# The first convolution block staged with x, the normalization in the tail of the projections, row copies on ScalarE

## The chip, the cores and the metric

The kernel runs on one core of a Trainium2 chip. Its metric is the device time of one execution in microseconds (us); lower is better. The engines are named as in the profile: PE is TensorE (PEld its weight loads), DVE is VectorE, ACT is ScalarE, POOL is GpSimd, and SP is SyncE, which issues most of the transfers. A row such as "L322 DVE ... x354 | 480.8, 1408" names a line of the kernel, its engine, what it writes and reads, how many instructions there were, their busy time in us and the mean of one in ns.

## The reference, cut to what matters

One layer of a decoder works on 2048 prompt tokens and 32 sample tokens (8 sequences of 4), 1024 wide, in fp32. The normalized input is multiplied by one wide matrix; its columns feed three branches: windowed attention (q, k, v, 12 heads of 64), a convolution branch (u) and cross-attention into 256 memory tokens (qc), besides gates. What the change touches:

```
h = _rmsnorm(x, g_pre) @ w_in
qa, ka, va, za, ub, zb, qc, zc, gt = split(h)
...
k_rows, v_rows = ka, va                                  # outputs too, row by row
glu  = ub[..., :768] * sigmoid(ub[..., 768:])
full = concatenate([hist_conv, glu], axis=1)             # 30 rows of history
conv = depthwise_conv(full, conv_w)  + conv_b            # width 31, 768 channels
ob   = silu(_layernorm(conv, ln_g, ln_b))                # over the 768 channels
conv_state = full[:, -30:]
```

The branch outputs are gated, projected, merged and projected once more. The layer also returns the key and value rows and the convolution's last 30 rows.

## The kernel before

**Layout and precision.** Tokens lie along the free axis, channels along the 128 partitions. x is kept in SBUF transposed, as eight slices of 128 channels, each split into a high and a low part. A weight block is 1024 x 128; it arrives as one 512 KB transfer (`load_w`, L145), and POOL splits it into `whi` and `wlo` (`split_pool`, L55 and L56). The raw, high and low tiles have two buffers each, so the split of the next block can begin when the first matmuls of the running block no longer need the tiles of the one before it. `gemm` (L160 to L168) makes three matmuls per slice: high by high, high by low, low by high, 24 for one piece.

**Pieces.** The 2080 tokens are cut into six pieces (`CHUNKS`: 384, 384, 384, 384, 256 and 288 columns). One weight block times six pieces is a block of the first phase: 144 matmuls. The product of a piece lies in one of four PSUM tiles `g`.

**First phase (`phase_a1`, L173).** `stage_x` (L104) brings x in six groups of three or two token tiles through the pool `xst` (seven buffers): a load by SP, squares on ScalarE, a square root, a scaling on VectorE (L127), transposes on PE (L132), and the split into high and low by ScalarE and VectorE (L135, L136). While this goes on, two blocks of q run piece by piece behind it. After the staging come the convolution's taps and the bias rows. Then six rounds follow, each a convolution block u and three blocks out of the list of k, v, q and qc, and at the end what is left of the list.

- A projection block (`blk_x`, L224; `chunk`, L229) copies each piece from PSUM by ScalarE into a staging tile `st` (L239, three buffers) and stores it by SP (L248). For k and v `rows_out` (L250) also transposes the piece back on PE, VectorE copies the rows out of PSUM (L260, and the sample rows L264), and SP stores them.
- A convolution block (`blk_u`, L268) loads 30 rows of history, transposes them into `GS` (L279, L281), multiplies the gate columns (tanh on ScalarE into `gate`, L290), then the value columns, and VectorE multiplies the two into `G` (L298; samples L303). `G` and `GS` have two buffers each in the pool `cnv`.
- `conv` (L309) then runs on VectorE: one L313, 59 L322 per block in `acc`, each a multiplication by one tap with an addition, besides the sample part (L331 to L334), the state rows (L338 to L351), and one store of `acc` to the scratch `d_c`. It is written at a lower priority (`later(LAG)`, 900 instructions), so that it falls between the work of the following blocks.

**What sets the order.** A planner takes the program's instructions with their priorities, which follow the order in which they are written unless `later` shifts them, and with its own durations puts them in one queue per engine. On the chip each engine goes through its queue in that order, and waits where an operand or a buffer is not there yet.

**Memory phase (`memory`, L884).** It computes keys and values of the 256 memory tokens (`memory_kv`, L905, eight weight blocks), the cross-attention and the sample parts. Into this phase the LayerNorm of the convolution branch is woven: `conv_norm` (L655) is a generator of nine steps of 256 columns, one per memory block, the last one behind them. A step loads six slices of `d_c` (one 128 x 1536 tile), sums over them on VectorE (`tensor_reduce`, L665), sums over partitions by a matmul with ones (L667), subtracts the mean (L668), squares on ScalarE (L671), sums again (L673, L675), makes 1/sqrt (L677, then L63 to L68: a square root on ScalarE, then a reciprocal and one correction on VectorE), scales (L679), applies `ln_g` and `ln_b` on POOL (six L681), takes tanh on ScalarE (L684), finishes the swish on VectorE (L685) and stores to `d_actb`.

**Filler.** From the end of the first phase the gate blocks (`sweep`, L1075: za, zb, zc, gt, PSUM tiles `gg`) run at the lowest priority wherever PE has room: through the memory phase, the attention of 12 heads and beyond it. Their weights are loaded from ScalarE's queue. Their tanh or swish is L243, or L245 with L246 on VectorE. The last phase (`phase_c`, L1103) gates, projects and merges.

Of the kernel before, what the change touches and what calls it, by code (L numbers as in the profile page):

```python
# [26 lines left out]
EARLY = 1  # L27
IN_COLS = 9472
# [9 lines left out]
class K:  # L38
# [134 lines left out]
    def phase_a1(self, wp, blocks=None):  # L173
        tc, nc, I, O = self.tc, self.nc, self.I, self.O
        with tc.tile_pool(name="x12", side="right", bufs=1) as xpool, \
# [4 lines left out]
                tc.tile_pool(name="pst", side="right", bufs=3, space=PSUM, reuse_waits="tile") as pst:  # L180
# [17 lines left out]
            with tc.tile_pool(name="cnv", side="right", bufs=1, reuse_waits="tile") as cnv:  # L198
                ws.append(self.load_w(wp, self.win(CQ + 128), 8, rp=self.wr))
                for cs, js in [(c, j) for c in (CHUNKS[:1], CHUNKS[1:2], CHUNKS[2:3], CHUNKS[3:4], CHUNKS[4:]) for j in range(2)]:  # L200
                    for s, n in cs:
                        self.chunk("q", js, s, n, ws[js], stg, psg, "g", pst)
                order = []
                rest = [("k", j) for j in range(6)] + [("v", j) for j in range(6)] + \
                       [("q", j) for j in range(2, 6)] + [("qc", j) for j in range(4)]
                for j in range(6):
                    order += [("u", j)] + rest[:3]
                    rest = rest[3:]
                order += rest
                for kind, j in order:  # L210
                    if blocks is not None and (kind, j) not in blocks:
                        continue
                    if kind == "u":
                        gs = self.blk_u(j, wp, stg, cnv, psg, pst)
# [7 lines left out]
                assert not out  # L222
                self.early = {("za", j): self.load_w(wp, self.win(CZA + 128 * j), 8, rp=self.wr) for j in range(EARLY)}
    def blk_x(self, kind, j, wp, stg, psg, pst):  # L224
        w = self.load_w(wp, self.win(self.BASE[kind] + j * 128), 8, rp=self.wr)
        for s, n in CHUNKS:
            self.chunk(kind, j, s, n, w, stg, psg, "g", pst)

# [21 lines left out]
    def rows_out(self, kind, j, s, n, st, stg, pst):  # L250
# [9 lines left out]
        nc.vector.tensor_copy(ro[:, :nt, :], p[:, :nt * 128].rearrange("p (t c) -> p t c", c=128))  # L260
# [7 lines left out]
    def blk_u(self, j, wp, stg, cnv, psg, pst):  # L268
        nc, I, O = self.nc, self.I, self.O
        G = cnv.tile([128, 16, 130], F32, name="G", bufs=2)  # L270
        GS = cnv.tile([128, 8, 34], F32, name="GS", bufs=2)
        nc.gpsimd.memset(G[:, :, 0:2], 0.0)

        st_in = cnv.tile([120, 2, 128], F32, name="st_in")
# [9 lines left out]

        w = self.load_w(wp, self.win(CUB + EB + j * 128), 8, rp=self.wr)
# [6 lines left out]
        for s, n in CHUNKS:  # L292
            th = gate[:, s:s + n]
            pa = psg.tile([128, 512], F32, name="g")
            self.gemm(pa[:, :n], w, [self.x_at(k, s, n) for k in range(8)])
            m = min(n, S - s)
            r0 = s // 128
            nc.vector.scalar_tensor_tensor(G[:, r0:r0 + m // 128, 2:130],  # L298
                                           th[:, :m].rearrange("p (r i) -> p r i", i=128), 1.0,
                                           pa[:, :m].rearrange("p (r i) -> p r i", i=128),  # L300
                                           op0=ALU.add, op1=ALU.mult)
            if m < n:
                nc.vector.scalar_tensor_tensor(GS[:, :, 30:34],  # L303
                                               th[:, m:n].rearrange("p (b t) -> p b t", t=4), 1.0,
                                               pa[:, m:n].rearrange("p (b t) -> p b t", t=4),
# [1002 lines left out]
```

## Time and profile before

| what | value |
|---|---|
| time, median of 3 runs | 3155.59 us (3150.18 to 3156.21) |
| profiled execution | 3154.4 us, span 3152.6 us |
| mean granted TensorE clock | 0.979 |
| busy share of PE, DVE, ACT, POOL | 95%, 64%, 36%, 43% |
| HBM traffic | 455 MB, mean 144 GB/s |
| first phase | from the start to the first filler matmul at 868.7 us |

The span runs from the first to the last instruction. Busy time of an engine leaves out its waits; matmuls are pipelined, and a "busy" PE at a lowered clock does less in the same time. The views by stretches therefore give the granted clock beside the busy time. The view of waits names for each idle time of PE the operation that ended it.

### The profile page before, as it was taken

The page shows a single profiled execution, that of the slowest core. Times are in us where ns is not written, and L with a number is a line of the kernel's source. Part 1 is how long each engine was busy: PE and PEld are TensorE (multiplying, and loading weights), DVE is VectorE, ACT ScalarE, POOL GpSimd, SP SyncE. Part 2 cuts the span into 40 slices and gives each one's busy share as a digit, 9 for nine tenths or more (in the row PEclk, how much of TensorE's full clock was granted, in tenths as well). Part 3 has the DMA queues.
Part 4 walks back from the last instruction along what each step waited for, and adds up shares of the span by engine and source line. Part 5 has one row for each costly group of instructions (what it writes and reads, how often), then busy time and mean ns, then how long its engine had stood idle before and what let it go on. Part 6 is the DMA issues. An engine that isn't in the chain of part 4 may idle for free.

```text
span 3152.6 us, 55374 instructions
## 1 busy us (share of the span) xinstructions
PE 3000.2 (95%) x20705; PEld 2839.9 (90%) x20705; DVE 2014.8 (64%) x3734; ACT 1124.2 (36%) x2835; POOL 1350.4 (43%) x1048
## 2 busy tenths in 40 slices
PE   7999999999987999999999999989899979999998
PEld 6899999999987999998999999989898967787897
DVE  5297797796677926465546766666656457556563
ACT  5010010010132433243437575656565523222221
POOL 0121221142356537444256565667676433233240
PEclk9899999999999999999999999999999989999999
DMA  7232222211265454477454656576555487657561
GB/s 250 85 103 80 80 60 61 63 62 50 81 182 167 135 153 144 147 219 239 151 139 116 161 123 163 128 185 150 156 143 152 109 279 227 223 168 227 161 197 53
DMA packets 532218, 454.66 MB, mean 144 GB/s; under 512 B 118191, under 2 KB 458581, under 8 KB 531137
## 3 DMA queue, kind: packets, MB, share of 16 engines
q1 hardware_dynamic: 357502, 335.36, 36.2%
q10 hardware_dynamic: 169840, 105.02, 11.7%
q0 software_dynamic: 4608, 10.75, 1.2%
q8 instruction: 164, 2.69, 0.4%
q14 instruction: 104, 0.85, 0.1%
HBM read 332.96 MB, written 118.04 MB: 143 GB/s over the span
## 4 chain that ended last, share of the span: by engine, by line
PE 70%; DMA 12%; DVE 7%; issue 4%; POOL 3%; ACT 2%; SPq 1%; ACTq 0%; DVEq 0%; POOLq 0%
PE g L166 8%; PE g L167 8%; PE g L168 8%; PE gg L166 6%; PE gg L168 6%; PE gg L167 6%; PE pg L168 3%; PE pg L166 3%; PE pg L167 3%; PE pt L571 2%; DMA cb<-d_cf 2%; PE y L1180 2%; PE y L1179 2%; PE y L1178 2%; PE o L598 1%
## 5 line engine op out<-in xcount | busy, mean ns | idle before, releaser
L166 PE MATMUL gg<-x0h,whi 128*128 128x256 f32 (+1 forms) x2560 | 747.9, 292 | 25.9 <-DVE st L246 12.2
L168 PE MATMUL gg<-x0h,wlo 128*128 128x256 f32 (+1 forms) x2560 | 741.8, 290 | 0.1
L167 PE MATMUL gg<-x0l,whi 128*128 128x256 f32 (+1 forms) x2560 | 741.1, 290 | 0.0
L55 POOL TENSOR_SCALAR whi<-wraw 128x1024 fp32r<-128x1024 f32 x162 | 242.7, 1500 | 928.5 <-PE g L167 524.1
L166 PEld LDWEIGHTS gg<-x0h,whi 128*128 128x128 f32 x2560 | 493.2, 193 | 35.0 <-DVE st L246 13.7
L167 PEld LDWEIGHTS gg<-x0l,whi 128*128 128x128 f32 x2560 | 493.5, 193 | 2.2 <-issue 0.5
L168 PEld LDWEIGHTS gg<-x0h,wlo 128*128 128x128 f32 x2560 | 493.2, 193 | 2.2 <-POOL wlo L56 0.3
L322 DVE SCALAR_TENSOR_TENSOR acc<-G,cw,acc 128x1536 f32<-128x1536 f32 (+15 forms) x354 | 480.8, 1408 | 0.3
L56 POOL TENSOR_TENSOR wlo<-wraw,whi 128x1024 fp32r<-128x1024 f32 x162 | 417.0, 2575 | 9.4 <-PE gg L168 0.2
L155 POOL TENSOR_TENSOR clo<-craw,chi 128x768 fp32r<-128x768 f32 (+1 forms) x96 | 174.1, 1815 | 346.0 <-ACT chi L154 329.8
L627 ACT ACTIVATE P<-T,stm 128x128 f32<-128x128 f32 (+1 forms) x576 | 260.8, 455 | 141.0 <-DVE stm L625 94.8
L239 ACT ACTIVATE st<-g 128x384 f32<-128x384 f32 (+1 forms) x132 | 60.2, 461 | 570.7 <-PE g L168 550.7
L166 PE MATMUL pg<-ac,chi 128*128 128x512 f32 (+1 forms) x640 | 229.4, 359 | 16.6 <-ACT chi L154 8.7
L625 DVE CUSTOM_DVE_ANT_0 T<-s,bias 128x128 f32<-128x128 f32 (+1 forms) x576 | 191.5, 357 | 80.8 <-PE s L617 47.0
L167 PE MATMUL pg<-ac,chi 128*128 128x512 f32 (+1 forms) x640 | 228.8, 358 | 6.3 <-DVE ac L1198 6.3
L168 PE MATMUL pg<-ac,clo 128*128 128x512 f32 (+1 forms) x640 | 227.6, 357 | 3.6 <-POOL clo L155 3.6
L576 DVE TENSOR_TENSOR pl<-pt,ph 128x512 fp32r<-128x512 f32 x240 | 155.6, 652 | 52.4 <-ACT ph L575 48.9
L168 PE MATMUL g<-x0h,wlo 128*128 128x384 f32 x544 | 184.3, 339 | 2.9 <-POOL wlo L56 2.9
L166 PE MATMUL g<-x0h,whi 128*128 128x384 f32 x544 | 183.6, 338 | 2.6 <-ACT st L239 2.3
L167 PE MATMUL g<-x1l,whi 128*128 128x384 f32 x544 | 186.0, 342 | 0.0
L167 PE MATMUL g<-x0l,whi 128*128 128x384 f32 x544 | 185.8, 342 | 0.0
L168 PE MATMUL g<-x1h,wlo 128*128 128x384 f32 x544 | 185.8, 342 | 0.0
(330 smaller groups left out, 7425.0 us busy)
## 6 DMA issues: line engine op xcount, KB each, us to landing
wraw<-in_w_in ACTq DMA_DIRECT2D x119, 512.0 KB
d_g<-st ACTq DMA_DIRECT2D x168, 128.0 KB
cb<-d_cf SPq DMA_DIRECT2D x72, 256.0 KB
g<-d_g SPq DMA_DIRECT2D x72, 256.0 KB
wraw<-in_w_in SPq DMA_DIRECT2D x35, 512.0 KB
kvc<-in_cache_k_win SPq DMA_DIRECT2D x8, 1536.0 KB
kvc<-in_cache_v_win SPq DMA_DIRECT2D x8, 1536.0 KB
raw<-d_q SPq DMA_DIRECT2D x48, 256.0 KB
```

The lines of the kernel that those rows point to most:

```text
L55: nc.gpsimd.tensor_scalar(hi, raw, 1.0, 1.0, op0=ALU.mult, op1=ALU.mult)
L56: nc.gpsimd.tensor_sub(lo, raw, hi.bitcast(F32))
L155: nc.gpsimd.tensor_sub(lo, raw, hi.bitcast(F32))
L166: nc.tensor.matmul(ps, hi[:, k, :], h, start=k == 0, stop=False)
L167: nc.tensor.matmul(ps, hi[:, k, :], l, start=False, stop=False)
L168: nc.tensor.matmul(ps, lo[:, k, :], h, start=False, stop=k == kb - 1)
L322: nc.vector.scalar_tensor_tensor(a3[:, lo:hi], G[:, src:src + hi - lo, 2 - m:130 - m], w, a3[:, lo:hi], op0=ALU.mult, op1=ALU.add)
L571: nc.tensor.transpose(t[:, 128 * x:128 * x + 128], pc, self.ident)
L576: nc.vector.tensor_tensor(pl[:, :w], t[:, :w], ph[:, :w].bitcast(F32), op=ALU.subtract)
L625: nc.vector.tensor_tensor_reduce(sc[:, :w], t[:, o:o + w], bias[:, 256 - w:256], 1.0, 3.0e38, ALU.add, ALU.min, m)
L627: nc.scalar.activation(P[:, o:o + w], sc[:, :w], AF.Exp, bias=m, scale=-1.0, accum_out=self.stl[:, col:col + 1])
L1178: nc.tensor.matmul(y[:m, c, :], ah[:, ts_], bh[:, cs], start=k == 0, stop=False)
```

## The change

It has four edits.

1. **The first convolution block goes with the staging of x.** In place of the two q blocks, the gate and value columns of u0 are multiplied piece by piece as x arrives. Its tanh goes to a staging tile `st` in place of `gate`. `xst` has six buffers in place of seven. `G` and `GS` live in two pools of one buffer each, one of them opened ahead of the staging; blocks take them in turn (`gated`).
2. **The order.** After u0 its convolution follows at the lower priority as before, then u1 with two blocks of the list, u2 with two, and so on to u5. Twelve blocks (v4, v5, six q, four qc) are left for the end: 72 pieces. The history rows are written by `states`, and the two zero columns of `G` are cleared by POOL at the first value piece.
3. **The normalization** leaves the memory phase. It gets a step after piece 28 of the last 72 and after every fifth from there (28, 33, ..., 68: nine steps). Its tiles are the convolution's: `G` and `GS` of both pools, `acc` and `gate`; its PSUM tiles are those of the transposes (`tr`). The sums over six slices are additions (five of 256 columns for the mean; one of 768 and two of 256 for the squares) in place of the two `tensor_reduce`.
4. **Row copies.** The copy of key and value rows out of PSUM (L260) is done by ScalarE in place of VectorE; the small copy of sample rows (L264) stays.

```diff
-            with tc.tile_pool(name="xst", side="right", bufs=7) as xst:
+            g0 = ctx.enter_context(tc.tile_pool(name="cng", side="right", bufs=1, reuse_waits="tile"))
+            with tc.tile_pool(name="xst", side="right", bufs=6) as xst:
...
-                ws = [self.load_w(wp, self.win(CQ), 8, rp=self.wr)]
+                ws = [self.load_w(wp, self.win(CUB + EB), 8, rp=self.wr)]
...
-                ws.append(self.load_w(wp, self.win(CQ + 128), 8, rp=self.wr))
-                for cs, js in [(c, j) for c in (CHUNKS[:1], CHUNKS[1:2], CHUNKS[2:3], CHUNKS[3:4], CHUNKS[4:]) for j in range(2)]:
-                    for s, n in cs:
-                        self.chunk("q", js, s, n, ws[js], stg, psg, "g", pst)
+                self.gpools = (g0, cnv)
+                ws.append(self.load_w(wp, self.win(CUB), 8, rp=self.wr))
+                first = self.gated(0)
+                for s, n in CHUNKS:
+                    pb = psg.tile([128, 512], F32, name="g")
+                    self.gemm(pb[:, :n], ws[0], [self.x_at(k, s, n) for k in range(8)])
+                    th = stg.tile([128, 384], F32, name="st")
+                    nc.scalar.activation(th[:, :n], pb[:, :n], AF.Tanh, scale=0.5)
+                    self.values(*first, s, n, ws[1], th, psg)
...
-                       [("q", j) for j in range(2, 6)] + [("qc", j) for j in range(4)]
+                       [("q", j) for j in range(6)] + [("qc", j) for j in range(4)]
                 for j in range(6):
-                    order += [("u", j)] + rest[:3]
-                    rest = rest[3:]
+                    order += [("u", j)] + (rest[:2] if j else [])
+                    rest = rest[2:] if j else rest
                 order += rest
+                ln = self.conv_norm(cnv, pst)
+                self.ticks = 0
+                def tick():
+                    self.ticks += 1
+                    if self.ticks >= NORM0 and (self.ticks - NORM0) % NORM1 == 0:
+                        next(ln, 0)
...
-                        self.blk_x(kind, j, wp, stg, psg, pst)
+                        self.blk_x(kind, j, wp, stg, psg, pst, tick if (kind, j) in rest else None)
...
+                for _ in ln:
+                    pass
...
-        nc.vector.tensor_copy(ro[:, :nt, :], p[:, :nt * 128].rearrange("p (t c) -> p t c", c=128))
+        nc.scalar.activation(ro[:, :nt, :], p[:, :nt * 128].rearrange("p (t c) -> p t c", c=128), AF.Copy)
...
+    def gated(self, j):
+        pool = self.gpools[j % 2]
+        G = pool.tile([128, 16, 130], F32, name="G")
+        GS = pool.tile([128, 8, 34], F32, name="GS")
+        return G, GS
...
+    def values(self, G, GS, s, n, w, th, psg):
+        nc = self.nc
+        pa = psg.tile([128, 512], F32, name="g")
+        self.gemm(pa[:, :n], w, [self.x_at(k, s, n) for k in range(8)])
...
+        if s == 0:
+            nc.gpsimd.memset(G[:, :, 0:2], 0.0)
+        nc.vector.scalar_tensor_tensor(G[:, r0:r0 + m // 128, 2:130],
...
-    def conv_norm(self, lp, ps):
+    def conv_norm(self, cnv, ps):
...
-            x = lp.tile([128, 6, W], F32, name="c", bufs=3)[:, :, :n]
+            G, GS = self.gated(s // W)
+            x = six(G.rearrange("p r i -> p (r i)"))
...
-            nc.vector.tensor_reduce(sm, x.rearrange("p j n -> p n j"), axis=AX.X, op=ALU.add)
-            p = ps.tile([128, 512], F32, name="str")[:, :n]
+            sm = GS.rearrange("p b w -> p (b w)")[:, :n]
+            nc.vector.tensor_add(sm, x[:, 0], x[:, 1])
+            for j in range(2, 6):
+                nc.vector.tensor_add(sm, sm, x[:, j])
+            p = ps.tile([128, 512], F32, name="tr")[:, :n]
...
-            nc.vector.tensor_reduce(sm, sq.rearrange("p j n -> p n j"), axis=AX.X, op=ALU.add)
-            p = ps.tile([128, 512], F32, name="sco")[:, :n]
-            nc.tensor.matmul(p, ones, sm, start=True, stop=True)
+            nc.vector.tensor_add(sq[:, 0:3], sq[:, 0:3], sq[:, 3:6])
+            nc.vector.tensor_add(sq[:, 0], sq[:, 0], sq[:, 1])
+            nc.vector.tensor_add(sq[:, 0], sq[:, 0], sq[:, 2])
+            p = ps.tile([128, 512], F32, name="tr")[:, :n]
+            nc.tensor.matmul(p, ones, sq[:, 0], start=True, stop=True)
...
-            rs = self.rsqrt(lp, var, [128, W], "ln", n)
+            nc.scalar.activation(sd, var, AF.Sqrt)
+            nc.vector.reciprocal(r, sd)
...
-                KT, VV = self.memory_kv(mp, kp, wp, ps, ln)
-            for _ in ln:
-                pass
+                KT, VV = self.memory_kv(mp, kp, wp, ps)
...
-            next(ln, 0)
```

More of the change, by code (lines that the diff above doesn't have):

```diff
@@ L1 @@
-from contextlib import contextmanager
+from contextlib import ExitStack, contextmanager
 import numpy as np
@@ L179, in phase_a1 @@
                 tc.tile_pool(name="psg", side="right", bufs=4, space=PSUM, reuse_waits="tile") as psg, \
-                tc.tile_pool(name="pst", side="right", bufs=3, space=PSUM, reuse_waits="tile") as pst:
+                tc.tile_pool(name="pst", side="right", bufs=3, space=PSUM, reuse_waits="tile") as pst, \
+                ExitStack() as ctx:
             for th in (1, 2):
@@ L213, in phase_a1 @@
                     if kind == "u":
-                        gs = self.blk_u(j, wp, stg, cnv, psg, pst)
+                        gs = first if j == 0 else self.gated(j)
+                        self.states(j, cnv, pst, gs[1])
+                        if j:
+                            self.blk_u(j, wp, cnv, psg, *gs)
                         with self.later(LAG):
@@ L266, in rows_out, with states @@
             nc.sync.dma_start(o[:, j * 128:(j + 1) * 128], ro[:NS, nt, :])
[L268 to L272, printed above, removed]
+    def gated(self, j):
[3 more added lines that the diff above has]
+        return G, GS
+    def states(self, j, cnv, pst, GS):
+        nc, I = self.nc, self.I
         st_in = cnv.tile([120, 2, 128], F32, name="st_in")
@@ L292, in blk_u @@
         for s, n in CHUNKS:
[L293 to L300, printed above, removed]
-                                           op0=ALU.add, op1=ALU.mult)
[L302 to L305, printed above, removed]
-                                               op0=ALU.add, op1=ALU.mult)
-        return G, GS
+            self.values(G, GS, s, n, w, gate[:, s:s + n], psg)
+    def values(self, G, GS, s, n, w, th, psg):
+        nc = self.nc
+        pa = psg.tile([128, 512], F32, name="g")
+        self.gemm(pa[:, :n], w, [self.x_at(k, s, n) for k in range(8)])
+        m = min(n, S - s)
+        r0 = s // 128
+        if s == 0:
+            nc.gpsimd.memset(G[:, :, 0:2], 0.0)
+        nc.vector.scalar_tensor_tensor(G[:, r0:r0 + m // 128, 2:130],
+                                       th[:, :m].rearrange("p (r i) -> p r i", i=128), 1.0,
+                                       pa[:, :m].rearrange("p (r i) -> p r i", i=128),
+                                       op0=ALU.add, op1=ALU.mult)
+        if m < n:
+            nc.vector.scalar_tensor_tensor(GS[:, :, 30:34],
+                                           th[:, m:n].rearrange("p (b t) -> p b t", t=4), 1.0,
+                                           pa[:, m:n].rearrange("p (b t) -> p b t", t=4),
+                                           op0=ALU.add, op1=ALU.mult)
     def conv(self, j, cnv, pst, G, GS):
@@ L652, in o_out @@
             nc.vector.tensor_add(d, f(O), f(tmp))
-    def conv_norm(self, lp, ps):
+    def conv_norm(self, cnv, ps):
         nc = self.nc
-        ones = lp.tile([128, 128], F32, name="ones")
+        ones = cnv.tile([128, 128], F32, name="ones")
         nc.vector.memset(ones, 1.0)
@@ L682, in conv_norm @@
                                         op0=ALU.mult, op1=ALU.add)
-            t = lp.tile([128, 6, W], F32, name="sq", bufs=1)[:, :, :n]
+            t = six(gate)
             nc.scalar.activation(t, x, AF.Tanh, scale=0.5)
```

25 lines of the change are left out of this document (16 added, 9 removed).

## The prediction

> **What bounds the kernel now.** I read the page first, then engine busy time in stretches of 50 us, then TensorE's waits in the stretch that the stretches single out, then the groups of instructions there and in the first phase. The page's head:
>
> ```profile
> span 3152.6 us, 55374 instructions
> PE 3000.2 (95%) x20705; PEld 2839.9 (90%) x20705; DVE 2014.8 (64%) x3734; ACT 1124.2 (36%) x2835; POOL 1350.4 (43%) x1048
> ```
>
> TensorE (PE) is busy 95% of the span. The change removes no matmul, so the time can only move by TensorE's idle time and by the clock it is granted. Where both are bad, by stretches (columns: stretch, its length, busy time of PE, PEld, DVE, ACT and POOL, granted clock, DMA share, GB/s):
>
> ```profile
> 650.00:700.00 50.00, 44.79 (x283) 44.06 (x281) 49.93 (x42) 5.54 (x12) 31.27 (x4) 1.00 0.21 66
> 700.00:750.00 50.00, 50.00 (x321) 50.00 (x320) 24.49 (x23) 4.05 (x9) 7.48 (x4) 1.00 0.16 54
> ...
> 850.00:900.00 50.00, 39.66 (x245) 37.62 (x245) 24.11 (x30) 11.16 (x19) 13.46 (x8) 0.87 0.52 163
> 900.00:950.00 50.00, 45.02 (x370) 44.20 (x368) 40.40 (x39) 15.01 (x26) 31.82 (x31) 1.00 0.48 141
> 950.00:1000.00 50.00, 39.11 (x280) 37.40 (x280) 37.15 (x31) 14.86 (x22) 28.01 (x25) 0.86 0.50 148
> 1000.00:1050.00 50.00, 44.07 (x348) 42.32 (x349) 40.74 (x64) 20.46 (x42) 35.80 (x32) 1.00 0.62 199
> 1050.00:1100.00 50.00, 46.95 (x384) 45.81 (x383) 46.72 (x90) 23.29 (x57) 24.53 (x25) 1.00 0.40 122
> 1100.00:1150.00 50.00, 48.43 (x387) 47.27 (x386) 19.43 (x29) 20.34 (x33) 22.98 (x23) 1.00 0.52 158
> ...
> 2550.00:2600.00 50.00, 33.53 (x118) 24.66 (x117) 32.61 (x39) 18.09 (x25) 14.34 (x10) 0.83 0.91 298
> ```
>
> The six stretches from 850 to 1150 us, where the normalization runs, leave PE idle 300 − 263.2 = 36.8 us. Two of them also have a lowered clock: at most 39.66 × 0.13 + 39.11 × 0.14 = 10.6 us of slower matmuls. What PE waited for between 840 and 1160 us (total us, times, longest), and below the "..." one row of the same view over the whole program:
>
> ```profile
> PE sco L675 <- DVE sm L673: 14.9, 5, 9.0
> PE gg L166 <- DVE st L246: 10.1, 9, 1.8
> PE str L667 <- DVE sm L665: 4.5, 5, 1.4
> PE gg L166 <- POOL whi L55: 3.9, 1, 3.9
> ...
> PE gg L166 <- DVE st L246: 12.2, 12, 1.8
> ```
>
> Rows 1 and 3 are the normalization's ones-matmuls waiting for VectorE's sums, 19.4 us. Row 2 is filler waiting for VectorE's gate step (L246): 10.1 of the program's 12.2 us of it fall in these 320 us, behind the normalization's long VectorE operations. Its groups there:
>
> ```profile
> L685 DVE SCALAR_TENSOR_TENSOR c<-sq,c 128x1536 f32<-128x1536 f32 (+1 forms) x9 | 35.3, 3926 | 21.9 <-ACT sq L684 21.9
> L681 POOL TENSOR_SCALAR c<-c,vecs 128x256 f32<-128x256 f32 (+1 forms) x54 | 28.4, 542 | 12.0 <-DVE c L679 6.7 <-DVE sl L1005 5.4
> L673 DVE TENSOR_REDUCE sm<-sq 128x256 f32<-128x1536 f32 (+1 forms) x9 | 23.5, 2613 | 9.9 <-ACT sq L671 9.9
> L665 DVE TENSOR_REDUCE sm<-c 128x256 f32<-128x1536 f32 (+1 forms) x9 | 23.2, 2577 | 0.7 <-DMA c<-d_c 0.7
> L63 ACT ACT_TABLE_LOAD x9 | 11.5, 1283 | 17.1 <-DVE var L677 11.8 <-DVE ml L926 4.8 <-ACT st L243 0.4
> L675 PE MATMUL sco<-sm,ones 128*128 128x256 f32 (+1 forms) x18 | 7.0, 479 | 14.9 <-DVE sm L673 14.9
> L667 PE MATMUL str<-sm,ones 128*128 128x256 f32 (+1 forms) x18 | 6.8, 463 | 6.1 <-DVE sm L665 4.5 <-DVE mss L917 1.5
> ```
>
> **Part one: the normalization leaves the memory phase.** Gone there are 19.4 us of direct waits and the 10.1 behind them, 29.5 together, and of the 10.6 us of clock I take 6, because the wait for the first filler weights (row 4) is there too and stays. That is −35.5; the bounds are −19.4 (only the direct waits go) and −47.4 (all 36.8 idle and all 10.6 of clock).
>
> The nine steps come back in the tail of the first phase. The 7.0 + 6.8 us of matmuls move and are neither saved nor added. Per step five 256-wide additions replace L665's 2.6 us and three additions replace L673's; the trace has no such addition, and between 128x256 on POOL at 542 ns and the reductions themselves the chain gets from about 1 us shorter to nothing. VectorE hides it: the convolutions are then over, and a step's VectorE work, 35.3 + 23.5 + 23.2 over nine plus the short ones, some 13 us, fits between steps five pieces apart, about 20 us. What is not hidden is the order: ScalarE's square root with its table load (1283 ns) and POOL's six L681 (3.3 us) are in each chain, PE takes its queue in order, and behind a ones-matmul that comes too early stands a whole piece of projection, and behind that the weights' buffers. Bounds: 0, and the 29.5 us of before; I take 13, two thirds of the direct 19.4, since no L246 stands behind VectorE there and the tail's stretch 700 to 750 leaves VectorE half free.
>
> The tail has to begin after the last convolution. That one ends in the row below at 839.4 us now. With one projection block less per convolution (24.7 us each by the two rows at 298.04 and 322.73 further down) and a first block that goes with x, it should end near 839 − 5 × 24.7 − 46 = 670. The filler starts at 868.7 us, and 45 of the 72 pieces (3.9 us each: two blocks of six between the rows at 777.05 and 823.00 below) lie from the first step to there, so the first step falls at about 693: some 20 us of margin, in which the 1 MB store of that convolution also has to land.
>
> ```profile
> 829.74 9.64 DVE L322 SCALAR_TENSOR_TENSOR acc<-G,cw,acc 128x640 f32<-128x640 f32 x8
> ...
> L166 PE MATMUL gg<-x0h,whi x24: 279/283/385, 868.7 to 879.7; 128*128 128x256 f32 x24
> ```
>
> **Part two: denser convolutions, and the row copies on ScalarE.** VectorE's groups in the first phase (110 to 870 us):
>
> ```profile
> L322 DVE SCALAR_TENSOR_TENSOR acc<-G,cw,acc 128x1536 f32<-128x1536 f32 (+15 forms) x354 | 480.8, 1408 | 0.3
> L260 DVE COPY ro<-tr 128x384 f32<-128x384 f32 (+1 forms) x72 | 35.7, 496 | 0.0
> L331 DVE TENSOR_TENSOR prod<-GS,cw 128x124 f32<-128x124 f32 x48 | 21.4, 504 | 0.0
> L298 DVE SCALAR_TENSOR_TENSOR G<-gate,g 128x384 f32<-128x384 f32 (+1 forms) x36 | 18.4, 510 | 146.5 <-PE g L168 146.5
> ```
>
> One convolution with its gating is (480.8 + 21.4 + 18.4) / 6 = 86.8 us, some 90 with the small ones. A cycle is now four blocks instead of five, 2 × 24.7 + 2 × 23.0 = 95 us. With the copies (12 × 0.5 = 6 us) VectorE would not fit, without them it just does, with 5 us to spare. ScalarE takes them for nothing: it is busy 5.54 us of 50 above, and the matmul behind L239 has three more PSUM tiles.
>
> But the copies did one thing more. POOL splits each block's weights (L55, then L56), and while VectorE runs L322 without a break, L55 does not get through (start, duration):
>
> ```profile
> 298.04 2.93 POOL L55 TENSOR_SCALAR whi<-wraw 128x1024 fp32r<-128x1024 f32 x1 [20.30 <-PE g L167]
> ...
> 322.73 2.69 POOL L55 TENSOR_SCALAR whi<-wraw 128x1024 fp32r<-128x1024 f32 x1 [18.43 <-PE g L167]
> ...
> 657.08 21.74 POOL L55 TENSOR_SCALAR whi<-wraw 128x1024 fp32r<-128x1024 f32 x1 [18.76 <-PE g L167]
> ...
> 683.12 2.95 POOL L55 TENSOR_SCALAR whi<-wraw 128x1024 fp32r<-128x1024 f32 x1
> ...
> 777.05 7.79 POOL L55 TENSOR_SCALAR whi<-wraw 128x1024 fp32r<-128x1024 f32 x1 [18.42 <-PE g L167]
> ...
> 823.00 17.29 POOL L55 TENSOR_SCALAR whi<-wraw 128x1024 fp32r<-128x1024 f32 x1 [17.00 <-PE g L167]
> ```
> ```profile
> 655.38 52.16 DVE L322 SCALAR_TENSOR_TENSOR acc<-G,cw,acc 128x768 f32<-128x768 f32 x38
> ...
> 683.21 0.45 PE L168 MATMUL g<-x0h,wlo 128*128 128x384 f32 x1 [2.95 <-POOL wlo L56]
> ```
>
> In the key and value blocks, with six copies each, L55 takes under 3 us; in the query blocks of now, which have none, it took 21.74, 2.95, 7.79 and 17.29. The 21.74 made PE late: 2.95 us at its first wlo, so that a wait up to 18.8 would have cost nothing, and with what followed from it idle 50 − 44.79 = 5.2 us in that stretch. The change makes every key and value block under a convolution like that. With about three weight splits per cycle that now lie in a run of L322 without a gap, for five cycles and a bit, some 16 splits are exposed; at one long wait in four of 5.2 us that is 21 us. The small operations of the convolution (L331 and its neighbours) can break the runs as the copies did, which the query blocks at 657 no longer had, since they were done by then. I take 8. Bounds: 0, and half of the splits, 42.
>
> The Trainium skill, "SBUF — State Buffer", section "SBUF: two separate sides", says that VectorE and GpSimd share one port pair as an exclusive lock, held for a whole instruction, by a VectorE operation with two SBUF inputs as well. The trace agrees, with 21.74 us of L55 behind 38 of L322. By that rule an operation with one input, or one that reads PSUM, opens the lock as the copies do.
>
> **Part three: the first block with x.** Two gemms per piece stay two gemms. Six buffers in place of seven hold just two groups of three tiles; the seventh let one tile of the next group go a release earlier. ScalarE gets a tanh between the square roots, so up to nine table loads of 1283 ns in its chain to the next group's scale. PE waited in this stretch for the scaled tiles already:
>
> ```profile
> PE tr L132 <- DVE xt L127: 9.9, 2, 6.0
> ...
> 48.84 1.28 SPq L117 DMA_DIRECT2D xt<-in_x_prompt  x3
> ```
>
> The bounds are 0 and 12 (all loads in the open, 11.5, or this wait doubled); I take +5: in four groups the third tile is issued behind two others of its batch (1.28 us for three), some 1 us late, and one table load in the open. The Trainium skill, "ScalarE: Activation LUTs", section "What ACT_TABLE_LOAD costs", counts a switch of tables at about 2.66 us with its drain; by it, an estimate, nine would be 24 us and this term about 11, not 5. The trace shows the 1283 ns and no row for a drain.
>
> **Part four: the end.** Filler that the shorter memory phase does not use is left for the time after attention. There the last row of the stretches has PE idle 16.5 us of 50. I take −6 between 0 and −16.5.
>
> **The sum.** −35.5 + 13 + 8 + 5 − 6 = −15.5 us against the profiled execution's own 3154.4, which gives 3138.9. That execution is 1.2 us under the median shown, 3155.6, so the forecast is **3140 us** on the median.
>
> **The rivals.**
>
> 1. *POOL is shut out* (slower). The place is the whole of the convolutions' time; the price is 5.2 us per long L55; it decides from about the eighth long wait on. Half of the 16 splits give 42 us in place of 8: −15.5 + 34 = +18.5, so 3174. For it: 21.74 and 17.29 of four. Against it: the 2.95 inside the same run of L322, and the small operations.
> 2. *The stalls move along* (no change). PE waits for the nine steps in the tail as it did in the memory phase, 29.5 instead of 13: −15.5 + 16.5 = +1, so 3157. For it: the chain of each step is as long as before, and the 20 us margin before the first step; a convolution that ends later puts PE behind it. Against it: VectorE is free there, and the fillers' L246 is not.
> 3. *A larger gain*. The tail costs 3, starvation 2, the start 2, and the end gives all 16.5: −35.5 + 3 + 2 + 2 − 16.5 = −45, so 3111. For it: VectorE is half free in the tail. Against it: the end's stretch has DMA at 0.91, which filler does not shorten.
>
> **How the numbers follow.** The forecast has 0.45, the first rival 0.17, the second 0.20, the third 0.18. The forecast's own range is 3132 to 3154: a third of each term's way to its bounds, added in squares, −8 and +14. A difference of 0.2%, 6.3 us, is about what can be told from no change. Faster (under 3149) holds the third rival and most of the forecast, 0.60; no change the second and the rest of the forecast, less what of the second lies over 3162, 0.22; slower the first and that, 0.18. For 8 in 10 the range goes from 3110 to 3170: the far half of the third rival and the far half of the first lie outside.
>
> **What would show it.** Right: PE idle between the first filler and 250 us later falls from 36.8 to some 8 us; L55 stays under 18.8 us in nearly all blocks; the ones-matmuls' own waits in the tail sum to 13. Wrong: many L55 over 18.8 with PE waiting for wlo (rival one); PE's waits at the two ones-matmuls near 20 us again, or the first load of the normalization waiting for the last convolution's store (rival two); PE's wait for scaled tiles of x well over 9.9 us. The forecast fails as a whole if the memory phase shows other waits of the same size where the normalization was.

## The result and the profile after

The changed kernel takes 3132.2 us (median) beside 3153.8 us before (five executions of each): the ratio is 0.9938 with a 95% interval of 0.9915 to 0.996, some 20 us faster. One execution of the changed kernel took 9279.7 us and is left out of the ratio. Run again later (`e12_after_again`, further down) it took 3130.1 beside 3150.8, a ratio of 0.9937 (0.9918 to 0.9955). The profiled execution took 3126.5 us, the fastest of those compared (up to 3140.9), so the stages below are read against the 3154.4 of the profiled one before, 28 us more.

The head of the page after, and then busy time by stretches (columns as in the prediction):

```profile
span 3124.7 us, 55530 instructions
PE 2989.5 (96%) x20705; PEld 2831.7 (91%) x20705; DVE 1951.8 (62%) x3716; ACT 1166.3 (37%) x2917; POOL 1390.9 (45%) x1048
```
```profile
500.00:550.00 50.00, 47.08 (x297) 46.51 (x295) 50.00 (x45) 3.65 (x8) 24.66 (x5) 1.00 0.09 25
...
800.00:850.00 50.00, 46.25 (x288) 45.28 (x287) 33.04 (x36) 19.64 (x25) 17.48 (x18) 1.00 0.42 129
850.00:900.00 50.00, 49.86 (x328) 49.15 (x327) 30.55 (x53) 21.10 (x31) 12.85 (x21) 1.00 0.42 135
900.00:950.00 50.00, 42.86 (x331) 41.73 (x330) 15.58 (x29) 10.86 (x23) 39.67 (x29) 0.90 0.63 174
950.00:1000.00 50.00, 50.00 (x411) 49.29 (x410) 17.52 (x46) 13.35 (x39) 31.89 (x28) 1.00 0.51 154
1000.00:1050.00 50.00, 49.64 (x390) 48.02 (x388) 28.95 (x70) 21.51 (x58) 18.39 (x17) 1.00 0.47 146
1050.00:1100.00 50.00, 50.00 (x400) 47.42 (x399) 34.19 (x86) 20.53 (x61) 37.50 (x36) 1.00 0.51 154
...
2400.00:2450.00 50.00, 41.42 (x300) 40.39 (x299) 13.61 (x8) 6.34 (x15) 32.44 (x19) 0.93 0.86 237
...
2550.00:2600.00 50.00, 44.70 (x179) 33.98 (x179) 37.31 (x42) 17.55 (x25) 23.89 (x13) 0.97 0.91 294
```

The memory phase, in which PE was busy 39 to 48 us of 50, is full but for its first stretch. In return PE has small gaps under the convolutions and in the tail, and a new one near 2400, where attention ends. The rows below show what PE waited for in the changed kernel between 690 and 1160 us (besides two waits of 0.4 us) and, under the "...", between 110 and 690 us. Lines after L25 are numbered anew: L710 is the ones-matmul for the mean, once L667; L56 and L57 split the weights, once L55 and L56; L357 is the tap, once L322; L334 is the gating, once L298; L263 is the copy to `st` and L280 the transposes behind it, once L239 and L256; L270 is once L246.

```profile
PE tr L710 <- DVE GS L708: 5.9, 4, 2.1
PE tr L970 <- DVE mt L966: 6.7, 2, 5.9
...
PE g L167 <- DVE G L334: 4.8, 2, 3.4
PE tr L280 <- ACT st L263: 4.0, 4, 1.5
```

The taps of all convolutions and the filler's matmuls, by tile (count, shortest, median and longest in ns, first and last start in us):

```profile
L357 DVE SCALAR_TENSOR_TENSOR acc<-G,cw,acc x354: 327/1399/4293, 119.8 to 674.8; 128x1792 f32<-128x1792 f32 x12, 128x1664 f32<-128x1664 f32 x12, 128x1536 f32<-128x1536 f32 x12, 128x1408 f32<-128x1408 f32 x12
...
L167 PE MATMUL gg<-x0h,whi x2560: 274/283/582, 893.4 to 2532.4; 128*128 128x256 f32 x173, 128*128 128x288 f32 x24
```

The last tap starts at 674.8 us, the first filler matmul at 893.4.

**Losses by stage.** PE's work is nearly the same in every complete kernel here (span less losses is 2948 to 2956 us in the rows below), so I add up what it loses: its idle time, and its busy time multiplied by what is missing of the granted clock, over stretches of 10 us. The stages end at 110 us, at 690 us, and then at milestones of PE's own rows: the first filler matmul, the first matmul of the sample attention, the first and the last score of attention, and the first matmul of the last phase. In us:

| kernel | start | convolutions | tail | memory | sample | attention | filler after it | last phase | sum |
|---|---|---|---|---|---|---|---|---|---|
| before | 33.4 | 5.2 | 0.0 | 47.9 | 12.0 | 53.8 | 3.9 | 44.5 | 200.7 |
| after | 32.8 | 11.9 | 6.1 | 10.5 | 18.6 | 47.8 | 13.8 | 31.5 | 173.0 |
| after, second profile | 34.5 | 11.6 | 8.1 | 9.6 | 21.3 | 48.1 | 9.9 | 32.3 | 175.4 |
| e8: staging and order only | 32.6 | 12.4 | 0.0 | 46.5 | 22.0 | 48.9 | 7.3 | 43.7 | 213.3 |
| e5: all but the normalization's place | 33.7 | 11.7 | 0.0 | 45.4 | 21.0 | 53.8 | 6.1 | 46.8 | 218.4 |
| e1: all but the copies on ScalarE | 35.1 | 12.5 | 13.6 | 22.5 | 18.8 | 47.1 | 16.7 | 35.1 | 201.4 |
| e2: only the copies on ScalarE | 29.1 | 34.8 | 4.2 | 49.3 | 10.3 | 53.2 | 1.6 | 43.2 | 225.7 |

The two first rows differ by 27.7 us, and the spans by 27.9: the sum closes.

### The profile page after: what moved, and what is told of

It reads as the page before. It is cut to its first block, busy times and chain, and to the rows that moved or that the text cites. A ratio compares the mean times of both kernels' runs of the same rounds, so it can differ in the third digit from the quotient of the medians.

```text
span 3124.7 us, 55530 instructions
## 1 busy us (share of the span) xinstructions
PE 2989.5 (96%) x20705; PEld 2831.7 (91%) x20705; DVE 1951.8 (62%) x3716; ACT 1166.3 (37%) x2917; POOL 1390.9 (45%) x1048
## 3 DMA queue, kind: packets, MB, share of 16 engines
q10 hardware_dynamic: 169840, 105.02, 11.7%
## 4 chain that ended last, share of the span: by engine, by line
PE 54%; DMA 9%; DVE 3%; POOL 2%; issue 2%; ACT 1%; SPq 1%; ACTq 0%; DVEq 0%; POOLq 0%
PE gg L167 8%; PE gg L169 8%; PE gg L168 8%; PE pg L169 3%; PE pg L168 3%; PE pg L167 3%; PE pt L606 3%; PE y L1224 2%; PE y L1225 2%; PE y L1223 2%; DMA cb<-d_cf 2%; PE o L633 2%; PE s L651 2%; PE s L652 2%; PE o L632 2%
## 5 line engine op out<-in xcount | busy, mean ns | idle before, releaser
L56 POOL TENSOR_SCALAR whi<-wraw 128x1024 fp32r<-128x1024 f32 x162 | 285.3, 1762 | 821.8 <-PE g L168 467.6
L357 DVE SCALAR_TENSOR_TENSOR acc<-G,cw,acc 128x1536 f32<-128x1536 f32 (+15 forms) x354 | 479.2, 1413 | 0.2
L57 POOL TENSOR_TENSOR wlo<-wraw,whi 128x1024 fp32r<-128x1024 f32 x162 | 411.9, 2543 | 8.9
L167 PE MATMUL pg<-ac,chi 128*128 128x512 f32 (+1 forms) x640 | 227.4, 357 | 12.4 <-ACT chi L155 5.2
L167 PE MATMUL g<-x1h,whi 128*128 128x384 f32 x544 | 185.2, 344 | 1.1 <-ACT x1h L136 1.1
```

The source lines that it names most:

```text
L56: nc.gpsimd.tensor_scalar(hi, raw, 1.0, 1.0, op0=ALU.mult, op1=ALU.mult)
L57: nc.gpsimd.tensor_sub(lo, raw, hi.bitcast(F32))
L167: nc.tensor.matmul(ps, hi[:, k, :], h, start=k == 0, stop=False)
L357: nc.vector.scalar_tensor_tensor(a3[:, lo:hi], G[:, src:src + hi - lo, 2 - m:130 - m], w, a3[:, lo:hi], op0=ALU.mult, op1=ALU.add)
```

## The experiments

Each ratio is against the kernel before on the same chip.

**The changed kernel again.**

> The changed kernel once more, on the chip of the three runs beside it, with a second profile: 3132 us, 15 to 22 under the kernel before. Its losses by stage are to come out within a few us of the first profile; a stage that does not was chance there.

3130.1 us, 0.9937 (0.9918 to 0.9955). Its losses are in the third row of the table: every stage is within 4 us of the first profile. So a difference of 2 or 3 us in one stage says nothing here; one of 6 is more than these two profiles differ by.

**The parts, one at a time.** Three runs leave out one or two of the edits. The first has the normalization back in `memory`, with the code it had before:

```diff
-                ln = self.conv_norm(cnv, pst)
+                ln = iter(())
...
+            ln = self.conv_norm(lp, lps)
...
-                KT, VV = self.memory_kv(mp, kp, wp, ps)
+                KT, VV = self.memory_kv(mp, kp, wp, ps, ln)
+            for _ in ln:
+                pass
```

> The changed kernel with the normalization back in the memory phase, in the form it had before (tensor_reduce, its own buffers, a step per memory block); staging, order and copies as changed. Theory one (the place of the normalization is the gain): the memory phase loses its 35 to 40 us again and the tail saves 6, and with the changes further on that gives 15 to 30 us more than the changed kernel, 3147 to 3162 us. Theory two (the shorter cycle and the copies bring the gain): 3 to 10 us more than the changed kernel, 3135 to 3142.

3176.7 us, 1.0097 (1.0069 to 1.0125): slower than before, and 1.6% slower than the changed kernel. Theory one holds, with a size that was too small (3147 to 3162): the memory phase loses 45.4 in place of 10.5, and the last phase 46.8 in place of 31.5. The waits in its memory phase are the old ones:

```profile
PE gg L167 <- DVE st L270: 10.3, 4, 5.7
PE str L702 <- DVE sm L700: 8.5, 6, 2.1
PE sco L710 <- DVE sm L708: 7.5, 4, 3.5
```

The second has, on top of this, the row copies on VectorE again (the diff of `e1` below), so that only the staging and the order are left:

> Only the first two edits: u0 in the staging and the order of u with two blocks each; the normalization in the memory phase as before, row copies on VectorE. Theory one (the copies' 18 us in the changed kernel come from a convolution chain that ends after the first normalization step): without steps in the tail a late chain costs nothing, and this is within 5 us of the run with the copies on ScalarE and the normalization in the memory phase, and near the kernel before, 3147 to 3158. Theory two (copies on VectorE cost in the convolutions themselves): 12 to 20 us slower than that run, 3162 to 3175.

3168.7 us, 1.006 (1.0044 to 1.0076). It is 8 us faster than the run with the copies on ScalarE, a little more than the 5 of theory one, and nothing like the 12 to 20 slower of theory two. But both are above the kernel before: the first two edits alone cost 0.6%. Theory two had the time (3162 to 3175), but for another reason. By the table these two edits lose 7 us more under the convolutions and 10 in the sample part, where the wait for KTh (5.1 us) is longer than before, and the first filler matmul comes 10 us later.

The third is the changed kernel with the copies back:

```diff
-        nc.scalar.activation(ro[:, :nt, :], p[:, :nt * 128].rearrange("p (t c) -> p t c", c=128), AF.Copy)
+        nc.vector.tensor_copy(ro[:, :nt, :], p[:, :nt * 128].rearrange("p (t c) -> p t c", c=128))
```

> The changed kernel with the 72 row copies back on VectorE, all else as changed. Theory one (VectorE's room): in the changed trace VectorE is busy 45 to 50 us of every 50 between 150 and 650 us; 60 copies of 0.5 us under the convolutions add 30 us to a chain that has about 10 to spare, so the last convolution ends some 20 to 30 us after 677 us, the value blocks' L334 stand behind it and the first normalization step comes late: 5 to 20 us slower than the changed kernel, 3137 to 3152. Theory two (POOL's way in): the copies out of PSUM let POOL's split of the weights through, its longest waits of 9 to 14 us fall to 3, VectorE loses nothing: same as the changed kernel or up to 8 us faster, 3124 to 3132.

3150.3 us, 1.0006 (0.9993 to 1.0019): theory one. POOL's L56 does fall to 4 us and less in every block, and it does not help, since the loss under the convolutions stays (12.5 for 11.9). The chain is 36 us late, and the tail and the start of the memory phase pay (13.6 and 22.5 for 6.1 and 10.5). PE's waits from 110 to 1216 us, then the taps, the last one now at 711.2 us:

```profile
PE tr L970 <- DVE mt L966: 12.9, 2, 10.8
PE tr L710 <- DVE GS L708: 11.3, 3, 7.5
```
```profile
L357 DVE SCALAR_TENSOR_TENSOR acc<-G,cw,acc x354: 328/1399/4304, 123.3 to 711.2; 128x1792 f32<-128x1792 f32 x12, 128x1664 f32<-128x1664 f32 x12, 128x1536 f32<-128x1536 f32 x12, 128x1408 f32<-128x1408 f32 x12
```

So the copies on ScalarE gain 0.7% where the normalization stands behind the convolutions. Where it does not they seem to lose 0.4% (1.0097 against 1.006), but those two intervals overlap.

**The copies alone, in the kernel before.** The reverse of the last diff, and nothing else:

> The kernel before with the row copies on ScalarE and nothing else changed. Theory one: VectorE waits 146 us for values in that phase anyway, so nothing is gained, and the split of weights waits 9 to 14 us instead of 3 without reaching PE: 3154, within 5 us. Theory two (the first rival of the prediction): splits now wait for the end of a run of L322 and some of them over 18.8 us, so PE waits for weights in several key and value blocks: 10 to 40 us slower, 3164 to 3194.

3178.0 us, 1.0086 (1.0073 to 1.0099): theory two by the time, not by its mechanism. L55 is shut out for 20.4 us in each of the next three convolutions and 10.41 in the first (its 21.76 later was there before, too), but PE waits for weights only once, for 3.0 us, as it did before the edit (2.95). PE waits for ScalarE. The waits of PE between 110 and 900 us:

```profile
PE tr L256 <- ACT st L239: 28.5, 3, 9.8
PE g L168 <- POOL wlo L56: 3.0, 1, 3.0
```

One of the three, engine by engine (start, duration):

```profile
295.37 20.40 POOL L55 TENSOR_SCALAR whi<-wraw 128x1024 fp32r<-128x1024 f32 x1 [20.31 <-PE g L167]
315.86 4.25 POOL L56 TENSOR_TENSOR wlo<-wraw,whi 128x1024 fp32r<-128x1024 f32 x1
...
296.00 0.42 SPq L248 DMA_DIRECT2D d_k<-st  x1
320.13 0.38 SPq L150 DMA_DIRECT2D wraw<-in_w_in  x1
320.61 0.53 SPq L262 DMA_DIRECT2D out_k_win_p<-ro  x1
...
325.36 0.49 ACT L260 ACTIVATE ro<-tr 128x384 f32<-128x384 f32 x1 [15.76 <-DMA out_k_win_s<-ro]
325.75 0.93 ACT L239 ACTIVATE st<-g 128x384 f32<-128x384 f32 x2
...
326.29 0.90 PE L256 MATMUL tr<-ident,st 128*128 128x128 f32 x3 [9.81 <-ACT st L239]
...
302.62 0.27 DVE L264 COPY ro<-tr 32x128 f32<-32x128 f32 x1
302.83 24.34 DVE L322 SCALAR_TENSOR_TENSOR acc<-G,cw,acc 128x640 f32<-128x640 f32 x17
```

The split ends at 320.11. Until then it holds the raw weights' buffer, so the next weight load waits at the head of SP's queue (320.13), and every store behind it waits, too, from 296.42 on. The row tiles `ro` are not stored, so ScalarE stands at its copy for 15.76 us; the piece's own L239 is queued behind that copy, and PE needs its tile. While the copies were on VectorE, ScalarE's queue could not be stopped by `ro`.

**The same with the weight loads off SP's queue.**

```diff
-        w = self.load_w(wp, self.win(self.BASE[kind] + j * 128), 8, rp=self.wr)
+        w = self.load_w(wp, self.win(self.BASE[kind] + j * 128), 8, q=self.nc.gpsimd, rp=self.wr)
...
-        w = self.load_w(wp, self.win(CUB + EB + j * 128), 8, rp=self.wr)
+        w = self.load_w(wp, self.win(CUB + EB + j * 128), 8, q=self.nc.gpsimd, rp=self.wr)
...
-        w = self.load_w(wp, self.win(CUB + j * 128), 8, rp=self.wr)
+        w = self.load_w(wp, self.win(CUB + j * 128), 8, q=self.nc.gpsimd, rp=self.wr)
```

> The kernel before with row copies on ScalarE (the run that took 3178), and the weight loads of the first phase's blocks issued from POOL's queue in place of SP's. Theory one (the queue): a late split keeps the raw buffer, the next weight load waits for it at the head of SP's queue, and the stores behind it keep the tiles that ScalarE and then PE need; without that load on SP's queue the 28.5 us at the transposes' wait for ScalarE vanish, and the time is 3145 to 3158. Theory two (PE waits for the weights themselves, or ScalarE for VectorE): the waits stay and it is 3168 to 3180.

3163.8 us, 1.0046 (1.0031 to 1.0062). The 28.5 us are gone, and the loss under the convolutions is 5.9 in place of 34.8, near the 5.2 of the kernel before, although L55 is still shut out for 20.4 us three times. So the path through SP's queue is shown. The time lies 6 us above what theory one gave: the memory phase loses 54.6 in place of 49.3, and the three stages behind it 2 to 5 us more each; why is open. In the changed kernel the same edit was tried:

> The changed kernel with the weight loads of the first phase's blocks issued from POOL's queue. Theory one (the queue): of the 12 us lost between 110 and 690 us the 4 at the transposes' wait for ScalarE go, and a few with them: 2 to 8 us faster than the changed kernel, 3124 to 3130. Theory two (POOL pays for issuing, or a load that waits for POOL's turn comes late for PE): 3 to 15 us slower, 3135 to 3147.

3162.5 us, 1.0039 (1.0026 to 1.0052): slower, as theory two had it, but by 30 us over the changed kernel in place of 3 to 15, and not by its reason. The wait of 4.0 at the transposes goes. But one split is now shut out for 30.38 us (what it had waited for before that was PE, not its load), and PE waits for both of its results, 9.0 us: the prediction's first rival as it was written. Why that split came to stand behind a longer run of taps is open. The convolutions lose 21.3 us in place of 11.9; the rest of the 26.8 us by which the profiles' losses differ is spread over the other stages. PE between 110 and 690 us, and the split:

```profile
PE g L167 <- DVE G L334: 6.0, 2, 3.3
PE g L167 <- POOL whi L56: 5.7, 1, 5.7
PE g L169 <- POOL wlo L57: 3.3, 1, 3.3
```
```profile
601.92 30.38 POOL L56 TENSOR_SCALAR whi<-wraw 128x1024 fp32r<-128x1024 f32 x1 [10.61 <-PE g L168]
```

**How near the changed kernel is to that.** Its convolutions are written 700 in place of 900 instructions behind (`LAG = 700`):

> The changed kernel with convolutions written 700 instead of 900 instructions behind. Theory one (VectorE is full through the convolutions, so their order hardly matters): losses between 110 and 690 us stay near 12, within 5 us of the changed kernel. Theory two (the gating L334 that now stands behind a run of L357 for 4.8 us comes later still): 6 to 15 us slower, 3138 to 3147.

3156.4 us, 1.0017 (1.0004 to 1.0031): slower by about 25 us, more than either theory, and not by L334. It is the queue again: L56 is shut out for up to 25.33 us, the next weight load stands at the head of SP's queue for 26.7, ScalarE's copy waits 18.7 for the store of a row tile, and PE waits 25.4 us for ScalarE's tile (second fence, 110 to 1000 us).

```profile
277.57 25.33 POOL L56 TENSOR_SCALAR whi<-wraw 128x1024 fp32r<-128x1024 f32 x1 [20.39 <-PE g L168]
```
```profile
PE tr L280 <- ACT st L263: 25.4, 5, 12.8
```

**What the normalization itself costs.** Its steps only load and store their columns; the convolution branch goes on unnormalized. In the changed kernel, then in the kernel before:

```diff
             nc.sync.dma_start(x, self.d_c[:, :, s:s + n].rearrange("j p n -> p j n"))
+            if True:
+                nc.sync.dma_start(self.d_actb[:, :, s:s + n].rearrange("j p n -> p j n"), x)
+                yield
+                continue
```

> The changed kernel with the normalization's arithmetic left out: its steps only load their columns and store them to the scratch again, so the convolution branch goes on unnormalized. Theory one: the normalization costs in the tail its 13.8 us of matmuls and about 6 us of idle PE: 18 to 24 us faster than the changed kernel, 3108 to 3114. Theory two (it also sets the end of the phase and disturbs the first filler): 30 to 40 us faster, 3092 to 3102.

> The kernel before with the normalization's arithmetic left out, loads and stores kept. Theory one: in the memory phase it costs the 13.8 us of matmuls and the 30 to 37 us of stalls and clock that the prediction gave it: 43 to 51 us faster than before, 3103 to 3111, so that the move itself is worth the difference to the run on the changed kernel, about 28 us. Theory two (the stalls are the memory phase's own and come back with other names): 14 to 25 us faster, 3129 to 3140.

3127.5 (0.9917, 0.9905 to 0.993) and 3128.4 (0.9931, 0.9917 to 0.9944). Without the arithmetic both kernels take the same time within their intervals, so the difference between them comes with the normalization: it cost some 21 us before and costs some 5 after, a difference that the intervals of 0.9938 and 0.9917 do not part from nothing. Both expectations of the first missed: the tail's 6.1 us do go to 0.0, and 13.8 us of matmuls with them, but the sample part loses 30.1 in place of 18.6 and the last phase 36.4 in place of 31.5. Filler waits there for the next third of x, and PE for POOL's split of bias tiles:

```profile
PE gg L167 <- DMA x0h<-d_x: 9.2, 3, 8.5
PE pt L435 <- POOL pl L57: 7.3, 2, 6.0
```

In the second, theory two's 14 to 25 us was right: the memory phase still loses 26.7 of 47.9, mostly by waits that were not in the rows before, and the sample part 30.7 in place of 12.0. The memory phase's waits:

```profile
PE tr L947 <- ACT kt L939: 4.4, 2, 2.4
PE gg L166 <- DVE st L246: 4.3, 3, 1.9
PE tr L928 <- DVE mt L924: 3.3, 2, 3.0
```

**When the steps come.** `NORM0, NORM1 = 36, 4` and `22, 5` in place of `28, 5`:

> The changed kernel with the nine steps after pieces 36, 40, ..., 68: the first 31 us later, and 16 us apart in place of 20. Theory one (the tail's loss comes from the margin between the last convolution's store and the first step): the 5.9 us of waits at the ones-matmuls fall under 3 and the time is 3126 to 3132. Theory two (it comes from each step's chain, whose VectorE work is 13.4 us by the groups of the changed kernel's trace and fills a step of 16): the waits grow to 10 to 20 us, 3138 to 3148.

3149.4 us, 0.9996 (0.998 to 1.0012): theory two by the time and the waits, each a little over its range. The tail loses 30.4 in place of 6.1; PE's waits between 690 and 1000 us, and then the mean's matmuls of the changed kernel and of this one (two per step):

```profile
PE tr L719 <- DVE mrr L65: 11.6, 1, 11.6
PE tr L710 <- DVE GS L708: 9.9, 4, 8.1
PE gg L167 <- DVE gate L722: 4.0, 1, 4.0
PE tr L719 <- DVE acc L717: 3.2, 2, 2.7
```
```profile
L710 PE MATMUL tr<-GS,ones x18: 190/378/483, 712.6 to 880.8; 128*128 128x256 f32 x16, 128*128 128x32 f32 x2
...
L710 PE MATMUL tr<-GS,ones x18: 377/378/483, 740.9 to 908.8; 128*128 128x256 f32 x16, 128*128 128x32 f32 x2
```

But theory two's reason, VectorE's time, is not what the trace shows. VectorE is busy only 29 to 33 us of each 50 between 740 and 890. The nine steps take 168 us from the first to the last in both kernels, 21 us each, though they are written 20 us apart in one and 16 in the other. So it is the rest of the step's chain that keeps them apart: ScalarE, POOL, the transfers, or its tiles `acc` and `gate`, of which there is one each. Which of these was not tested. Up to 888 us, where the last projection piece ends, this kernel's tail loses 2.4 us. The other 28.0 are lost behind it: the last two steps are late there, and PE has no piece left to work on.

> The changed kernel with the nine steps after pieces 22, 27, ..., 62: the first 23 us earlier, before the last convolution's store has landed. Theory one (the margin of 20 us is needed, as in the prediction's second rival): PE waits for the first sum 10 to 20 us, 3140 to 3152. Theory two (the planner sees the late store and puts the matmul behind later pieces): waits of 3 to 8 us as now, and the first filler starts undisturbed, 3126 to 3134.

3144.2 us, 0.9975 (0.9963 to 0.9987). The time is theory one's, the waits are not: L710 waits 8.8 us in all, not 10 to 20, and the tail loses 14.8 in place of 6.1. The memory phase has 16.8 for 10.5 and the sample part 32.1 for 18.6; that earlier steps cause those two was not shown. No complete variant tried beats the changed kernel.

## Why the prediction was right

The forecast was 3140 in 3110 to 3170, and 3132 was measured. The terms sum to −15.5 us, the losses of the two profiles differ by −27.7; nearly all of that miss lies in two costs that were put too high, the tail and the start. By its terms, against the losses of the first two rows:

- **The memory phase, −35.5:** measured 47.9 to 10.5, −37.4. The three waits that the term was made of are gone from the rows. What is left is the start, where PE waits 6.7 us for the scaled memory tokens (L966). `e5` shows the cause: with the normalization put back the three waits return with 26.3 us and the memory phase loses 45.4. That the normalization's absence would free them all was too simple, as `e4` shows: in the order of before the phase without its arithmetic keeps 26.7, a gain of 21.2, and in the changed kernel (`e3`) it keeps 8.7. So the term came out in full only with the other edits, which it did not count on; that its size fits is in part luck. Which of the edits does it was not separated.
- **The tail, +13:** measured +6.1 (8.1 in the second profile), half. The mean's wait (L710) is 5.9 us in four; the second sum's is nothing. VectorE has room, some 13 us per step in 21. What has none is the step's whole chain, as `e9` shows: steps written 16 us apart still come 21 us apart, run out behind the last piece and lose 30. The prediction asked only whether VectorE's 13 us fit into 20. (It took a piece as 3.9 us; by its two rows it is 3.8.)
- **Starvation of POOL, +8:** measured +6.7, by another path, so that the size fits by luck. L56 was shut out for 8 to 14 us nine times and never to the 18.8 at which PE would have missed its weights. The prediction's 18.8 us were read from a wait for weights, and so are too high a bound for a split that costs nothing: `e2` and `e6` show that a long split first blocks SP's queue, then ScalarE, then PE. The changed kernel pays 4.0 us on that path and 4.8 where the gating L334 stands behind the taps. The prediction's reason for a small value, that small operations break the runs, is what the trace shows, with other operations than the L331 that it named. Of the 14.17 us below, 1.05 is the split's own time (last POOL row), so it got in at 532.94, as the gating L334 started, which reads PSUM. Of the nine waits four end in this way with L334, four with the small copy of sample rows out of PSUM (L288, once L264; the first POOL and the first DVE row below), and one between two taps. The 21.74 us of the prediction lie behind only a part of the run of 38 L322 shown there: the split ended at 678.82, the run at 707.54.

```profile
469.96 13.07 POOL L56 TENSOR_SCALAR whi<-wraw 128x1024 fp32r<-128x1024 f32 x1 [18.18 <-PE g L168]
...
519.82 14.17 POOL L56 TENSOR_SCALAR whi<-wraw 128x1024 fp32r<-128x1024 f32 x1 [18.08 <-PE g L168]
...
695.94 1.05 POOL L56 TENSOR_SCALAR whi<-wraw 128x1024 fp32r<-128x1024 f32 x1 [15.71 <-PE g L168]
...
482.04 0.27 DVE L288 COPY ro<-tr 32x128 f32<-32x128 f32 x1
...
513.47 19.61 DVE L357 SCALAR_TENSOR_TENSOR acc<-G,cw,acc 128x1280 f32<-128x1280 f32 x17
533.00 0.54 DVE L334 SCALAR_TENSOR_TENSOR G<-gate,g 128x384 f32<-128x384 f32 x1
```

- **The copies for nothing:** wrong as a general statement, though nearly right in the changed kernel, where they cost the 4.0 us above and gain more. In the kernel before they cost 0.9%. The step that failed is "ScalarE takes them for nothing: it is busy 5.54 us of 50": a free engine was counted, and not what its in-order queue would wait for (a store, behind a load, behind POOL).
- **VectorE's fit, 90 of 95 us:** right, and stronger than stated. `e1` shows it: with the copies back the chain ends 36 us later and the whole gain is lost.
- **The start, +5:** measured −0.6. In these 110 us ScalarE made eight more table loads than before (ten in the two groups below against two), and no loss at PE came of it. By the Trainium skill, "ScalarE: Activation LUTs", section "What ACT_TABLE_LOAD costs", the estimate was 24 us of ScalarE for nine. The trace has 1283 ns each, and in nine of the ten only 1.30 to 1.32 us lie between the end of the instruction before the load and the start of the one behind it, so here the measurement decides.

```profile
L64 ACT ACT_TABLE_LOAD x5 | 6.4, 1283 | 0.1
L210 ACT ACT_TABLE_LOAD x5 | 6.4, 1283 | 0.1
```

- **The end, −6:** the last phase −13.0, the filler stage +9.9, together −3.1. The prediction had only the first. More filler after attention covers the last phase's start, where PE is busy 44.70 of 50 us in place of 33.53, and loses by itself, with PE at 41.42 of 50 and 0.93 of the clock where attention ends.
- **Not in the sum:** the sample part +6.6 and attention −6.0, which cancel.

The first rival's mechanism is real. `e2` and `e11` are kernels in which it decides, through SP's queue, at splits of 20 us and more; in `e7` PE waits for the weights themselves, as the rival was written. It failed here since the changed order's runs of taps are broken in time, with 14 us as the longest wait; 200 instructions of lag less were enough to bring it out. The second rival would have needed the tail to lose 29.5 us; `e9` loses that much, though behind the last piece and not at each step. That the first two edits cost 0.6% by themselves (`e8`) was not foreseen. The start, where I had put the cost, shows nothing; the convolutions lose 7.2 us more and the sample part 10.0, with some 5 back elsewhere, and what in the order makes the sample part worse is open.

## What to carry to other kernels

Read an edit's parts together before judging one: the copies on ScalarE change the time by −0.7% in the changed kernel and by +0.9% in the kernel before. An engine with idle time is free only if its queue cannot be stopped by the new instruction's buffers; follow each buffer to the store that frees it, and that store to the head of its queue. A long serial block is cheapest where a step's whole chain, not only one engine's share of it, keeps up with the distance between steps (here no closer than 21 us, of which VectorE has some 13), and where PE has independent work behind each of its waits, the last one too.

## What the runs showed of the hardware

POOL seldom gets in between two taps of VectorE. In the kernel before with the copies on ScalarE, L55 waited three times for 20.4 us behind back-to-back L322. Most often a short operation that reads PSUM lets it in: eight of the nine waits of 8 to 14 us in the changed kernel end as one starts (L334 or L288). But such a read is not enough by itself: the copy L264 at 302.62 lies inside the wait from 295.37 shown above and did not end it. Less the 1.05 us of a free one, that split got in at 314.72, between two L322 and with no read of PSUM near. The Trainium skill, "SBUF — State Buffer", section "Who interferes with whom", holds that whoever issues first has the shared ports for one instruction. This wait spans many instructions of VectorE, so the rule alone does not give its length. What decides which gap lets POOL in was not settled.

Executions of one kernel spread more than the differences between stages: 3126 to 3141 us for the changed one. The 0.6% is clear only over several executions, and the one pair of profiles overstates the gain by a third (28 for some 21 us).
